# Two-layer RWKV-7 and stick-breaking trunk: another substitution, RWKV's keys in whole rows, memory block moved, new order

## The chip, the cores and the metric

One core of one Trainium2 chip runs the whole program, one launch. The time is the device time of that launch in microseconds (us), the median of several runs. TensorE is called PE here, its weight loads PEld, VectorE DVE, ScalarE ACT, GpSimd POOL and SyncE SP.

## The reference, cut to what matters

256 tokens of 1024 channels go through two layers. Each layer is a gated FFN, a mixer with cross-attention to 256 memory tokens, and a second FFN, each closed by a layer norm. The mixer of layer 0 is RWKV-7, that of layer 1 stick-breaking attention.

```python
# layer i
x = LN(alpha * x + 0.5 * swiglu_1(x))            # (silu(x @ w_gate) * (x @ w_up)) @ w_down, D_FF = 2816
p = x @ W_in[i]                                  # token-mixer columns | memory-query columns
h = concat(mixer(p_mix), memory_attention(p_memq, memK, memV))
x = LN(alpha * x + h @ W_out[i])
x = LN(alpha * x + 0.5 * swiglu_2(x))

mem_kv = mem @ w_mem_kv                          # once, 1024 -> 256 keys | 256 values; 4 heads of 64
memory_attention: softmax(q @ memK.T / 8) @ memV

rwkv7:  kk = k * k_k;  kk = kk / |kk| per head;  k = k * (1 + (a - 1) * k_a)
        per token: state = state * w - (state @ kk) (kk * a)^T + v k^T;  out = state @ r
stick-breaking: att[t, s] = exp(log_sigmoid(z[t, s]) - sum over later s' < t of softplus(z[t, s'])), z = q k / 8
```

The kernel computes the token recurrence of RWKV in chunks of 64 tokens. Inside a chunk, the rows depend on each other through a unit lower triangular matrix of 64 x 64 per head, which has to be inverted. It does so for blocks of 16 x 16 by forward substitution, for 96 blocks at once (128 partitions, one block in each), and for the larger blocks by products on PE.

## The kernel before, in words

The tokens stand in two halves of 128 (`half 0`, `half 1`; tiles x_78 and x_79). All weights are streamed from HBM through SP's queue in pieces of 128 x 1024 (`piece`, ring `raw` of 8 tiles). Each piece is split in two numbers of reduced precision: ACT copies it to a `hi` tile, DVE subtracts to get `lo` (`lo = raw - hi`), both in rings of 9 tiles. A product is then three matmuls (`mm3`): hi by hi, lo by hi, hi by lo. In the rows, `hi_7r`, `lo_8r` and the like are such pieces, xTh and xTl the turned activations in two parts.

An FFN column block is 256 of the 2816 hidden columns (`ffn_block`, 11 of them). It is "alone" when it is computed for one half only (24 matmuls of 512 columns for gate and up, 12 for down, 2 transpositions), or for both halves at once from one load of its weights (96 matmuls of 256 columns, 24 of 512 for down). PSUM banks: ps_2, ps_3 for transpositions ("tp"), ps_29, ps_30 for gate and up and for projections ("gu"), ps_25 and ps_26 the accumulators of half 0, ps_27 and ps_28 of half 1; the mixers also use the accumulator banks.

What runs when: in layer 0, half 0 gets five alone columns and six shared ones, `memory_kv` stands among the first blocks, then the norm of half 0. While half 0 goes through the mixer, half 1 gets the columns that it still lacks (`alternate`, lag1); while half 1 goes through the mixer, half 0 is in its second FFN (lag2). The columns of the other half are thus what PE does while a mixer's chain is on DVE and ACT. HEAD, LAGS, FIRST, HOLD and TAIL say how many alone columns stand at each place.

The order on each engine is not that of the code. `Plan` records all operations, then `order` lists them: of the operations that can start soonest, within AHEAD ns of the soonest on that engine, the one with the lowest rank. The rank is the place in the code, plus WAIT per ns of waiting, plus SWITCH where ACT would need another table, plus TURN where PE changes its mode; operations of a mixer's chain stand BOOST earlier. `improve` then tries changed places, from a SEED.

`memory_kv` (L806) loads the memory rows of each half by itself, turns them in groups of four (two splits of 512 each), loads the pieces of w_mem_kv once and multiplies half after half in one gu bank.

In the mixer of layer 0, `rwkv` (L911), the tiles are named by slots: Sk, L, Lm, T, Tt, RB, Y, lb, qr, kn, vn, bn. Three places are touched:

- the keys (L984 on): `t1 = (a - 1) * k_a`, the square of `k * k_k`, and the two products with it, each as one operation per group of 128 channels (NT = 6 groups),
- the substitution (L1098 to L1102): for each k of 0 to 14 one product of column k of L with row k of the inverse T, into `lb`, and one subtraction from the rows below, in `Tt`. In the rows these are the pairs `lb<-Y,Tt` and `Tt<-Tt,lb`, with 15 to 64 elements per partition,
- the copy of the memory queries `mq`.

In layer 1, `stick` (L1267) computes the logarithms: Exp, then Ln of the sums, in the tiles L, Lm, T and Tt of 768 columns; then Exp of the attention in qr and Sk. Exp (with Tanh) and Ln lie in different activation tables, so ACT_TABLE_LOAD stands between them.

## Time and profile before

| | |
|---|---|
| median of 3 runs | 1133.79 us (1130.95 to 1135.38) |
| the profiled execution's own time | 1131.83 us |
| its span in the trace | 1129.7 us |
| PE busy | 1075.0 us (95%), 7013 instructions |
| PEld busy | 903.4 us (80%) |
| DVE busy | 955.0 us (85%), 1426 instructions |
| ACT busy | 739.3 us (65%), 991 instructions |
| read from HBM | 304.22 MB |
| chain that ended last | PE 83%, DVE 12%, issue 2%, DMA 2%, ACT 1% |

The span lies 2.1 us below the profiled execution's time; the trace doesn't show those. A busy time counts each instruction from start to end, and neighbours on an engine overlap a little, so a sum of durations is more than the time that they took. The norm statistics on DVE (BN_STATS) mark where one part ends: 170.8 us (half 0, FFN 1 of layer 0), 289.8 (half 1), 324.5 and 495.0 (both halves behind the mixer of layer 0), 589.7 and 624.4 (FFN 2), 769.4 and 854.1 (FFN 1 of layer 1), 886.6 and 976.0 (behind stick-breaking), 1099.7 and 1120.3 (FFN 2).

### The profile page before, as it was taken

What the parts mean: (1) busy time and instruction counts of PE and PEld (TensorE: products, weight loads), DVE (VectorE), ACT (ScalarE), POOL (GpSimd) and SP (SyncE); (2) the same over time, 40 slices, a digit from 0 to 9 for tenths busy, and PEclk for the clock granted to TensorE, in tenths of its full rate; (3) what the DMA queues carried; (4) which work ended last, traced back from release to release, by engine and by line L of the source; (5) the groups of instructions that cost most, each with busy time, mean ns of one, the idle gap of its engine ahead of it and who ended that gap; (6) DMA issues with size and microseconds to landing.
All of it is one profiled execution on the core that took longest, in us unless ns stands there. A gap on an engine that the chain in (4) does not pass through costs nothing.

```text
span 1129.7 us, 19266 instructions
## 1 busy us (share of the span) xinstructions
PE 1075.0 (95%) x7013; PEld 903.4 (80%) x7013; DVE 955.0 (85%) x1426; ACT 739.3 (65%) x991; POOL 2.7 (0%) x14
## 2 busy tenths in 40 slices
...
GB/s 357 252 183 379 246 237 294 304 191 116 178 219 305 150 160 258 260 350 365 329 289 329 301 286 257 234 242 261 383 258 266 342 292 271 373 342 326 277 277 113
DMA packets 214721, 306.55 MB, mean 271 GB/s; under 512 B 14004, under 2 KB 161632, under 8 KB 214626
## 3 DMA queue, kind: packets, MB, share of 16 engines
...
HBM read 304.22 MB, written 1.05 MB: 270 GB/s over the span
## 4 chain that ended last, share of the span: by engine, by line
PE 83%; DVE 12%; issue 2%; DMA 2%; ACT 1%; SPq 0%; DVEq 0%; ACTq 0%
PE ps_29r L562 25%; PE ps_30r L562 25%; PE ps_28r L562 7%; PE ps_27r L562 7%; PE ps_26r L562 7%; PE ps_25r L562 7%; PE ps_2r L562 3%; PE ps_3r L562 3%; DVE Y_377r L562 1%; DVE Tt_366r L562 1%; DVE lo_17r L562 1%; DVE lo_35r L562 1%; DVE lo_14r L562 1%; DVE lo_23r L562 1%; DMA raw_9r<-in_ffn_w_up_dram 1%
## 5 line engine op out<-in xcount | busy, mean ns | idle before, releaser
L562 ACT ACTIVATE h_32r<-ps_30r 128x256 f32<-128x256 f32 (+1 forms) x50 | 21.1, 421 | 30.3 <-PE ps_30r L562 29.8
L562 ACT ACTIVATE h_33r<-ps_29r 128x256 f32<-128x256 f32 (+1 forms) x48 | 20.0, 416 | 31.1 <-PE ps_29r L562 30.8
L562 DVE TENSOR_TENSOR h_33r<-h_33r,ps_29r 128x256 f32<-128x256 f32 x31 | 13.0, 418 | 11.3 <-ACT h_33r L562 11.1
L562 ACT ACTIVATE hi_19r<-raw_15r 128x1024 fp32r<-128x1024 f32 x13 | 13.7, 1056 | 9.3 <-DMA raw_15r<-in_w_out_dram 3.7
L562 PE MATMUL ps_30r<-hi_16r,xTh 128*128 128x512 f32 x46 | 19.7, 428 | 0.0
L562 PE MATMUL ps_30r<-lo_17r,xTh 128*128 128x512 f32 x46 | 18.1, 393 | 1.0 <-DVE lo_17r L562 1.0
L562 PE MATMUL ps_2r<-cst,x 128*128 128x128 f32 x48 | 9.2, 325 | 10.3 <-DMA x<-in_x_dram 5.3
L562 DVE TENSOR_TENSOR lo_20r<-raw_15r,hi_19r 128x1024 fp32r<-128x1024 f32 x13 | 15.8, 1216 | 3.4 <-ACT hi_19r L562 3.4
L562 PE MATMUL ps_30r<-hi_16r,xTl 128*128 128x512 f32 x46 | 18.0, 392 | 0.0
L562 PE MATMUL ps_29r<-lo_14r,xTh 128*128 128x512 f32 x26 | 10.9, 419 | 7.1 <-DVE lo_14r L562 7.1
L562 PE MATMUL ps_30r<-hi_10r,xTh 128*128 128x512 f32 (+1 forms) x42 | 17.5, 416 | 0.0
L562 PE MATMUL ps_29r<-hi_22r,xTh 128*128 128x512 f32 x42 | 17.4, 415 | 0.0
L562 ACT ACT_TABLE_LOAD x13 | 16.7, 1283 | 0.9 <-PEq L1451 0.7
L562 ACT ACTIVATE hi_16r<-raw_36r 128x1024 fp32r<-128x1024 f32 x10 | 10.6, 1057 | 10.2 <-DMA raw_36r<-in_w_out_dram 9.0
L562 ACT ACTIVATE hi_22r<-raw_9r 128x1024 fp32r<-128x1024 f32 x12 | 12.8, 1063 | 6.8 <-PE ps_30r L562 3.9
L562 DVE TENSOR_TENSOR lo_23r<-raw_9r,hi_22r 128x1024 fp32r<-128x1024 f32 x12 | 14.6, 1218 | 3.0 <-ACT hi_22r L562 3.0
L562 PE MATMUL ps_30r<-lo_11r,xTh 128*128 128x512 f32 (+1 forms) x42 | 16.5, 394 | 0.3 <-DVE lo_11r L562 0.3
L562 PE MATMUL ps_29r<-hi_22r,xTl 128*128 128x512 f32 x42 | 16.6, 396 | 0.0
L562 PE MATMUL ps_29r<-lo_23r,xTh 128*128 128x512 f32 x42 | 16.6, 395 | 0.0
L562 PE MATMUL ps_30r<-hi_10r,xTl 128*128 128x512 f32 (+1 forms) x42 | 16.5, 392 | 0.0
L562 PEld LDWEIGHTS ps_2r<-cst,x 128*128 128x128 f32 x48 | 6.8, 166 | 11.8 <-issue 5.3
L562 DVE TENSOR_TENSOR lo_35r<-raw_12r,hi_34r 128x1024 fp32r<-128x1024 f32 x12 | 14.6, 1216 | 1.9 <-ACT hi_34r L562 1.9
...
## 6 DMA issues: line engine op xcount, KB each, us to landing
...
```

What stands on the lines that cost most here:

```text
L562: fn(*[at(x) for x in a], **{n: at(x) for n, x in k.items()})
```

## The change

- **Numbers of the plan.** The numbers below; with LAGS[1] one column of layer 1's first FFN is shared instead of computed alone for each half.
- **The memory block.** `memory_kv` is a generator: it loads the memory rows into tiles of the ring `raw`, the turned parts lie in tiles of the rings `hi` and `lo`, and each piece of w_mem_kv serves both halves, with one gu bank each. It stands behind the norm of half 0 now, ahead of the RWKV chain of half 0.
- **Scale.** The 1/8 of the memory scores is in the copy of mq, and the maximum is taken with the sign turned, so one operation of two elements falls away per bank.
- **Keys.** The operations per group of 128 channels become one of 768 channels, with the factor broadcast; the square is taken of a product that DVE writes first.
- **Substitution.** The 16 x 16 block is taken as two 8 x 8 blocks on its diagonal, both in one operation: 7 steps of two operations. The block below the diagonal follows from two products of 8 x 8 x 8 (512 elements each) and two reductions.

```diff
-HEAD = 2
-LAGS = ((5, 9), (5, 8))
-FIRST = 1
+HEAD = 1
+LAGS = ((5, 9), (4, 8))
+FIRST = 2
-HOLD = (2, 3)
+HOLD = (3, 4)
-TAIL = (2, 2)
-AHEAD = dict(PE=100.0, DVE=400.0, ACT=0.0)
-WAIT = 0.98
-SWITCH = 49.0
-BOOST = 18.375
+TAIL = (1, 2)
+AHEAD = dict(PE=100.0, DVE=200.0, ACT=0.0)
+WAIT = 7.6832
+SWITCH = 68.6
+BOOST = 12.8625
-SEED = 201
-TURN = 11760.0
+SEED = 144
+TURN = 23520.0
...
     def memory_kv():
-        mT = []
+
+        rows = [new(wp, [P, D], F32, "raw", "mem", NRAW) for _ in range(NHALF)]
+        for hf, mt in enumerate(rows):
+            nc.in_turn("load", nc.sync.dma_start(mt, mem[0, half_sl(hf), :]))
+        o = [ps("gu") for _ in range(NHALF)]
+        for g in range(2):
+            mT = [new(wp, [P, D], F32R, n, "mT", NPIECE).rearrange("p (s k t) -> p s k t", s=NHALF, t=P) for n in ("hi", "lo")]
+            for hf, mt in enumerate(rows):
+                to_T(mt[:, g * 512:(g + 1) * 512], [t[:, hf] for t in mT], 0, 4)
+            for k, h, l in cols_pieces(w_mem_kv, 0, 512, (2 * g, 2 * g + 1)):
+                for hf in range(NHALF):
+                    mm3(o[hf], mT[0][:, hf, k % 4], mT[1][:, hf, k % 4], h, l, k == 0, k == KT - 1)
+                yield
...
-            nc.vector.tensor_reduce(rs[:, 0, two], scv, AX.X, ALU.max)
-            nc.vector.tensor_scalar(rs[:, 0, two], rs[:, 0, two], -0.125, None, ALU.mult)
+            nc.vector.tensor_reduce(rs[:, 0, two], scv, AX.X, ALU.max, negate=True)
...
-                nc.vector.tensor_copy(mq, ptv[:, nt:n // P])
+                nc.vector.tensor_scalar(mq, ptv[:, nt:n // P], 0.125, None, ALU.mult)
...
-        for j in range(NT):
-            nc.vector.tensor_scalar(t1[:, j], a[:, j], 1.0, k_a[:, j:j + 1], ALU.subtract, ALU.mult)
+        nc.vector.scalar_tensor_tensor(t1, a, 1.0, bc(k_a, 2, [P, NT, P]), ALU.subtract, ALU.mult)
...
-        for j in range(NT):
-            nc.scalar.activation(sq[:, 0, j], zk[:, j], AF.Square, scale=k_k[:, j:j + 1])
+        nc.vector.tensor_tensor(bt, zk, bc(k_k, 2, [P, NT, P]), ALU.mult)
+        nc.scalar.activation(sq[:, 0], bt, AF.Square)
...
-        for j in range(NT):
-            for dst, w in ((cv4(qr[:, :, 0]), e1[:, :, :, 0:C]), (cv4(bt), cv4(a))):
-                nc.vector.scalar_tensor_tensor(dst[:, j], cv4(zk)[:, j], k_k[:, j:j + 1], w[:, j], ALU.mult, ALU.mult)
+        nc.vector.tensor_mul(cv4(qr[:, :, 0]), cv4(bt), e1[:, :, :, 0:C])
+        nc.vector.tensor_mul(bt, bt, a)
...
-        for k in range(BLK - 1):
-            n = BLK - 1 - k
-            sh = [P, n, k + 1]
-            nc.vector.tensor_tensor(tmp[:, :n, :k + 1], bc(Lb[:, k, k + 1:], 2, sh), bc(Tn[:, k, :k + 1], 1, sh), ALU.mult)
-            nc.vector.tensor_tensor(Tn[:, k + 1:, :k + 1], Tn[:, k + 1:, :k + 1], tmp[:, :n, :k + 1], ALU.subtract)
+        for k in range(hb8 - 1):
+            n = hb8 - 1 - k
...
+            nc.vector.tensor_tensor(t, col, row, ALU.mult)
+            low = duo(Tn, k + 1, n, 0, k + 1)
+            nc.vector.tensor_tensor(low, low, t, ALU.subtract)
...
+        nc.vector.tensor_tensor(terms, bc(Lb[:, lo8, hi8].rearrange("p k i -> p i k"), 2, cube),
+                                bc(Tn[:, lo8, lo8].rearrange("p k j -> p j k"), 1, cube), ALU.mult)
+        nc.vector.tensor_reduce(w8, terms, AX.X, ALU.add, negate=True)
+        nc.vector.tensor_tensor(terms, bc(Tn[:, hi8, hi8], 2, cube), bc(w8.rearrange("p k j -> p j k"), 1, cube), ALU.mult)
+        nc.vector.tensor_reduce(Tn[:, hi8, lo8], terms, AX.X, ALU.add)
...
-            memory_kv()
...
+        if i == 0:
+            run(memory_kv())
```

The plan then orders the instructions anew. Three places follow, each with the order before and now.

DVE, memory block. Before, it stands among the first FFN columns; mT are the turned memory rows, memV and memKT the values and the turned keys.

```order
L562 TENSOR_TENSOR mT_58r<-ps_3r,mT_57r 128x512
L562 TENSOR_TENSOR lo_8r<-raw_9r,hi_7r 128x1024
L562 TENSOR_TENSOR lo_20r<-raw_12r,hi_19r 128x1024
L562 TENSOR_TENSOR mT_61r<-ps_2r,mT_60r 128x512
L562 TENSOR_TENSOR lo_23r<-raw_15r,hi_22r 128x1024
L562 TENSOR_TENSOR lo_11r<-raw_18r,hi_10r 128x1024
L562 COPY memV<-ps_30r 128x256
L562 TENSOR_TENSOR lo_14r<-raw_21r,hi_13r 128x1024
L562 TENSOR_TENSOR mT_65r<-ps_3r,mT_64r 128x512
L562 TENSOR_TENSOR mT_68r<-ps_2r,mT_67r 128x512
L562 COPY memKT<-ps_3r 128x2x128
```

Now it stands behind the norm of half 0; the turned rows are the four operations of 512 that read ps_2 and ps_3 and write lo_35 and lo_17.

```order
L562 TENSOR_TENSOR lo_41r<-raw_39r,hi_40r 128x1024
L562 TENSOR_TENSOR lo_23r<-raw_9r,hi_22r 128x1024
L562 TENSOR_TENSOR lo_14r<-raw_21r,hi_13r 128x1024
L562 TENSOR_TENSOR lo_35r<-ps_3r,hi_34r 128x512
L562 TENSOR_TENSOR lo_11r<-raw_15r,hi_10r 128x1024
L562 TENSOR_TENSOR lo_35r<-ps_2r,hi_34r 128x512
L562 TENSOR_TENSOR lo_17r<-ps_3r,hi_16r 128x512
L562 TENSOR_TENSOR lo_8r<-raw_18r,hi_7r 128x1024
L562 TENSOR_TENSOR lo_20r<-raw_36r,hi_19r 128x1024
L562 TENSOR_TENSOR lo_17r<-ps_2r,hi_16r 128x512
L562 TENSOR_TENSOR lo_38r<-raw_39r,hi_37r 128x1024
L562 TENSOR_TENSOR lo_35r<-raw_9r,hi_34r 128x1024
```

The same splits of turned rows stand in another part of the program, among splits of weight pieces.

DVE, substitution of half 1, from its first step. Before:

```order
L562 TENSOR_TENSOR lb_506r<-Y_377r,Tt_366r 128x15
L562 TENSOR_TENSOR Tt_366r<-Tt_366r,lb_506r 128x15
L562 TENSOR_TENSOR lb_506r<-Y_377r,Tt_366r 128x14x2
L562 TENSOR_TENSOR Tt_366r<-Tt_366r,lb_506r 128x14x2
L562 TENSOR_TENSOR lb_506r<-Y_377r,Tt_366r 128x13x3
L562 TENSOR_TENSOR Tt_366r<-Tt_366r,lb_506r 128x13x3
L562 TENSOR_TENSOR lb_506r<-Y_377r,Tt_366r 128x12x4
```

Now (slots have other numbers: lb is lb_480, Tt is Tt_340, Y is Y_351):

```order
L562 TENSOR_TENSOR lb_480r<-Y_351r,Tt_340r 128x14
L562 TENSOR_TENSOR lo_17r<-raw_18r,hi_16r 128x1024
L562 TENSOR_TENSOR Tt_340r<-Tt_340r,lb_480r 128x2x7
L562 SCALAR_TENSOR_TENSOR h_32r<-h_32r,ps_30r 128x256
L562 TENSOR_TENSOR lb_480r<-Y_351r,Tt_340r 128x24
L562 TENSOR_TENSOR lo_8r<-raw_24r,hi_7r 128x1024
L562 TENSOR_TENSOR Tt_340r<-Tt_340r,lb_480r 128x2x6x2
L562 TENSOR_TENSOR lo_11r<-raw_39r,hi_10r 128x1024
L562 TENSOR_TENSOR lb_480r<-Y_351r,Tt_340r 128x30
L562 TENSOR_TENSOR xTl<-ps_28r,xTh 128x2x128
L562 TENSOR_TENSOR Tt_340r<-Tt_340r,lb_480r 128x2x5x3
L562 TENSOR_TENSOR RB_344r<-ps_27r,cst 128x6x64
```

Before, the steps stand one behind the other; now another operation stands between every two of them.

ACT, the logarithms of stick-breaking half 1, up to the first Exp of the attention (qr). Before:

```order
L562 ACT_TABLE_LOAD
L562 ACTIVATE L_382r<-L_382r 128x768
L562 ACTIVATE Lm_367r<-Lm_367r 128x768
L562 ACTIVATE T_376r<-T_376r 128x768
L562 ACTIVATE hT_1974r<-ps_2r 128x256
L562 ACTIVATE hi_10r<-raw_21r 128x1024
L562 ACTIVATE Tt_366r<-Tt_366r 128x768
L562 ACTIVATE hi_7r<-raw_12r 128x1024
L562 ACTIVATE hi_22r<-raw_24r 128x1024
L562 ACTIVATE hi_13r<-raw_9r 128x1024
L562 ACT_TABLE_LOAD
L562 ACTIVATE qr_56r<-qr_56r 128x384 x2
```

Now (L is L_356, Lm is Lm_341, T is T_350, Tt is Tt_340, qr is qr_390):

```order
L562 ACT_TABLE_LOAD
L562 ACTIVATE L_356r<-L_356r 128x768
L562 ACT_TABLE_LOAD
L562 ACTIVATE T_350r<-T_350r 128x768
L562 ACT_TABLE_LOAD
L562 ACTIVATE Lm_341r<-Lm_341r 128x768
L562 ACTIVATE hi_13r<-raw_21r 128x1024
L562 ACTIVATE T_350r<-T_350r 128x768
L562 ACT_TABLE_LOAD
L562 ACTIVATE h_33r<-ps_29r 128x256
L562 ACTIVATE hi_22r<-raw_18r 128x1024
L562 ACT_TABLE_LOAD
```

Two table loads stand in the rows of before; in those of now there are five, and a sixth follows ahead of the first Exp of qr.

## Rows read from the trace of the kernel before

**Rows 1.** windows between norms: us, busy us by engine, PEclk, DMA share, GB/s

```profile
0.00:170.80 170.80, 160.71 (x987) 143.58 (x988) 111.25 (x127) 97.81 (x123) 1.63 (x9) 1.00 0.79 276
170.80:289.80 119.00, 111.43 (x1016) 89.90 (x1015) 114.56 (x236) 84.54 (x135) 0.20 (x1) 0.96 0.67 226
289.80:324.50 34.70, 25.87 (x275) 21.74 (x274) 33.15 (x68) 11.72 (x17) 0.64 (x3) 0.80 0.53 165
324.50:495.00 170.50, 158.43 (x1358) 125.66 (x1357) 163.30 (x305) 113.05 (x169) 0.21 (x1) 0.96 0.72 238
...
769.40:854.10 84.70, 83.36 (x405) 64.94 (x404) 77.91 (x106) 71.66 (x95) 0.00 (x0) 1.00 0.88 307
...
886.60:976.00 89.40, 89.29 (x472) 69.60 (x471) 87.26 (x118) 75.46 (x101) 0.00 (x0) 1.00 0.89 298
```

**Rows 2.** waits of PE, by releaser: us in total, times, longest us

```profile
PE ps_29r L562 <- DVE lo_14r L562: 7.1, 2, 6.0
PE ps_2r L562 <- DVE lb_506r L562: 5.9, 1, 5.9
PE ps_26r L562 <- DVE Y_377r L562: 5.8, 1, 5.8
...
PE ps_3r L562 <- DVE mT_65r L562: 2.1, 1, 2.1
```

**Rows 3.** chain that ended last, in order of time: start us, us, what

```profile
62.02 1.44 PE ps_30r L562 x12
...
65.25 5.47 PE ps_30r L562 x24
```

**Rows 4.** timeline of DVE, memory block: start us, us, operation

```profile
46.66 0.68 DVE L562 TENSOR_TENSOR mT_65r<-ps_3r,mT_64r 128x512 fp32r<-128x512 f32 x1
47.26 0.68 DVE L562 TENSOR_TENSOR mT_68r<-ps_2r,mT_67r 128x512 fp32r<-128x512 f32 x1
```

**Rows 5.** timeline of DVE, RWKV keys of half 0

```profile
206.66 0.34 DVE L562 SCALAR_TENSOR_TENSOR L_382r<-h_33r,vc,pT_399r 128x128 f32<-128x128 f32 x1
206.92 0.28 DVE L562 TENSOR_SCALAR Sk_381r<-RB_370r,vc 128x128 f32<-128x128 f32 x1
207.11 0.34 DVE L562 SCALAR_TENSOR_TENSOR L_382r<-h_33r,vc,pT_399r 128x128 f32<-128x128 f32 x1
...
213.21 0.96 DVE L562 TENSOR_TENSOR RB_370r<-RB_370r,Y_377r 128x768 f32<-128x768 f32 x1 [0.16 <-ACT Y_377r L562]
214.08 0.34 DVE L562 SCALAR_TENSOR_TENSOR qr_56r<-L_382r,vc,T_376r 128x128 f32<-128x128 f32 x1
```

**Rows 6.** timeline of DVE, substitution, half 0 and (from 402.86) half 1

```profile
255.99 0.18 DVE L562 TENSOR_TENSOR lb_506r<-Y_377r,Tt_366r 128x15 f32<-128x15 f32 x1
...
267.16 0.16 DVE L562 TENSOR_TENSOR Tt_366r<-Tt_366r,lb_506r 128x15 f32<-128x15 f32 x1
...
402.86 0.19 DVE L562 TENSOR_TENSOR lb_506r<-Y_377r,Tt_366r 128x15 f32<-128x15 f32 x1
...
407.78 0.22 DVE L562 TENSOR_TENSOR lb_506r<-Y_377r,Tt_366r 128x55 f32<-128x55 f32 x1
407.91 0.41 DVE L562 SCALAR_TENSOR_TENSOR h_33r<-h_33r,ps_29r 128x256 f32<-128x256 f32 x1
...
408.82 1.22 DVE L562 TENSOR_TENSOR lo_20r<-raw_21r,hi_19r 128x1024 fp32r<-128x1024 f32 x1
409.96 0.20 DVE L562 TENSOR_TENSOR Tt_366r<-Tt_366r,lb_506r 128x48 f32<-128x48 f32 x1
...
412.74 0.15 DVE L562 TENSOR_TENSOR Tt_366r<-Tt_366r,lb_506r 128x15 f32<-128x15 f32 x1
```

**Rows 7.** timeline of ACT, logarithms of stick-breaking half 1

```profile
931.66 1.28 ACT L562 ACT_TABLE_LOAD   x1
932.96 0.85 ACT L562 ACTIVATE L_382r<-L_382r 128x768 f32<-128x768 f32 x1
...
941.37 0.94 ACT L562 ACTIVATE qr_56r<-qr_56r 128x384 f32<-128x384 f32 x2
```

More of the change, by code (lines that the diff above doesn't have):

```diff
@@ L806, in memory_kv @@
     def memory_kv():
-        mT = []
-        for hf in range(NHALF):
-            mt = sl("qr", [P, D])
-            nc.sync.dma_start(mt, mem[0, half_sl(hf), :])
-            for g in range(2):
-                t = tuple(new(mp, [P, 4, P], F32R, n, "mT") for n in
-                          (("vn", "bn"), ("kn", "RB"), ("L", "Lm"), ("T", "Tt"))[2 * hf + g])
-                to_T(mt[:, g * 512:(g + 1) * 512], t, 0, 4)
-                mT.append(t)
-        pieces = cols_pieces(w_mem_kv, 0, 512)
-        for hf in range(NHALF):
-            a = ps("gu")
-            for k, h, l in pieces:
-                th, tl = mT[2 * hf + k // 4]
-                mm3(a, th[:, k % 4], tl[:, k % 4], h, l, k == 0, k == KT - 1)
+        rows = [new(wp, [P, D], F32, "raw", "mem", NRAW) for _ in range(NHALF)]
[10 more added lines that the diff above has]
+                yield
+        for hf in range(NHALF):
             mk = new(tp_, [P, MEMW], F32, "ta", "mk", 2)
-            nc.scalar.activation(mk, a[:, :MEMW], AF.Copy)
-            nc.vector.tensor_copy(memV[:, hf], a[:, MEMW:])
+            nc.scalar.activation(mk, o[hf][:, :MEMW], AF.Copy)
+            nc.vector.tensor_copy(memV[:, hf], o[hf][:, MEMW:])
             pt = ps("tp")
-            for j in range(2):
-                nc.tensor.transpose(pt[:, j * P:(j + 1) * P], mk[:, j * P:(j + 1) * P], ident)
+            with nc.together():
+                for j in range(2):
+                    nc.tensor.transpose(pt[:, j * P:(j + 1) * P], mk[:, j * P:(j + 1) * P], ident)
             nc.vector.tensor_copy(memKT[:, :, half_sl(hf)], pt[:, :2 * P].rearrange("p (j t) -> p j t", t=P))
@@ L841, in mem_attention @@
             two = slice(2 * p, 2 * p + 2)
-            nc.vector.tensor_reduce(rs[:, 0, two], scv, AX.X, ALU.max)
-            nc.vector.tensor_scalar(rs[:, 0, two], rs[:, 0, two], -0.125, None, ALU.mult)
+            nc.vector.tensor_reduce(rs[:, 0, two], scv, AX.X, ALU.max, negate=True)
             e = new(tp_, [P, 2, SEQ], F32, "ta", "e", 2)
             for j in range(2):
-                nc.scalar.activation(e[:, j], scv[:, j], AF.Exp, bias=rs[:, 0, 2 * p + j:2 * p + j + 1], scale=0.125,
+                nc.scalar.activation(e[:, j], scv[:, j], AF.Exp, bias=rs[:, 0, 2 * p + j:2 * p + j + 1],
                                      accum_out=rs[:, 1, 2 * p + j:2 * p + j + 1])
@@ L1080, in rwkv @@
         X, Tn = tt[:, :512], tt[:, 512:].rearrange("p (i j) -> p i j", j=BLK)
-        tmp = sl("lb")[:, :256].rearrange("p (i j) -> p i j", j=BLK)
+        scratch = sl("lb")
+        tmp = scratch[:, :256]
         D4 = v4(Dd, True)
```

12 lines of the change are left out of this document (11 added, 1 removed).

## The prediction

> **What bounds the kernel now.** I read the windows between the layer norms first, since the program runs from one norm of a half of x to the next and every edit lies between two known ones. The bounds of the windows are the starts of the norm statistics on DVE. Up to 170.8 us (the first FFN, all eleven columns for half 0 and six of them for half 1 too, and the memory block) PE is busy 160.7 us and DVE 111.3 [rows 1]: PE sets that time. From 170.8 to 495.0 us lie both RWKV halves. There DVE is busy 114.56 + 33.15 + 163.30 = 311.0 of 324.2 us (96%), PE 111.43 + 25.87 + 158.43 = 295.7: PE has 28.5 us without work, and where it idles most, from 289.8 to 324.5, its granted clock is .80 on average instead of 1.00 [rows 1]. The waits say the same: three long ones of PE, 6.0, 5.9 and 5.8 us, end with a DVE write (a weight split, the scratch lb of the substitution, Y of the triangular part), and one of 2.1 us with the split of the turned memory rows [rows 2]. So in the RWKV stretch DVE sets the time, and PE everywhere else: from 769.4 to 854.1 us PE is busy 83.36 of 84.70, from 886.6 to 976.0 us 89.29 of 89.40 [rows 1].
>
> **How I count.** For an engine that sets the time I take the number of its instructions between two norms in the order that the program prints, times the distance from start to start in the trace (neighbours overlap, so the duration of one is too much). On PE: 24 matmuls of 512 columns in 5.47 us, .2267 each, and 12 of 256 columns in 1.44 us, .120 each [rows 3]; a transposition of 128 columns I set at .108, a little under the .120. On DVE: a 1024 split 1.14 (408.82 to 409.96), a 512 one .60 (46.66 to 47.26), a 768 product .87 (213.21 to 214.08), a 128 scalar_tensor_tensor .26 and a 128 tensor_scalar .19 (206.66, 206.92, 207.11) [rows 4 to 6].
>
> **Up to the first norm: -15.4 us.** Memory_kv leaves this part, and the FFN columns in it stay as they are: up to the last matmul of half 0's first accumulator there are 312 instead of 360 matmuls of 512 columns, 26 instead of 46 transpositions of 128, and 576 of 256 columns in both. That is 48 x .2267 + 20 x .108 = 13.0, with rounding 13.1 us less on the engine that sets the time. The wait of PE for mT, 2.1 us [rows 2], goes with the block; with the slower matmuls just behind it I put 2.3. What hides this saving: only DVE (97 instead of 105 us of counted work, far below) and the weights' transfers, which lose 3 MB of the block too.
>
> **RWKV stretch: +6.5 us.** Here the block arrives, on the engine that sets the time. Counted from the first norm's statistics to half 1's second, DVE's work:
> - memory block: 4 splits of 1024 x 1.14 + 4 of 512 x .60 + 4 copies of 256 at .35 (an estimate between the .26 of 128 elements and the .60 of 512) = +8.4; two copies of mq become two tensor_scalar of the same size, nothing;
> - 2 more splits of 1024, of pieces whose matmuls lie elsewhere: +2.3;
> - RWKV keys, both halves: -12 tensor_scalar x .19 - 24 scalar_tensor_tensor of 128 x .26 + 8 operations of 768 x .87 = -2.3 - 6.2 + 7.0 = -1.5. The six Squares on ACT become one behind a new DVE product (ACT now waits for bt); ACT has 30% of its time free, and the next user is rn, so I put that at nothing: DVE's queue covers it with splits;
> - substitution, both halves: -60 small operations + 28, which at the distance of neighbours that don't depend on each other (.13, 407.78 to 407.91 [rows 6]) is -7.8 + 3.6; plus 4 products of 512 x .60 and 4 reductions to 64 of 512 elements. Such a reduction isn't in the trace; between .50 (its elements at the 768 row's .87) and .95, I take .61: +4.8. Sum +.6;
> - the rest (four negations of two elements gone, single gate operations that cross a norm) about 0.
>
> Sum +9.3: 298.3 us of counted work become 307.6. Before, 324.2 - 298.3 = 25.9 us were not work. Part of this is dependence: in the substitution each step reads the one ahead, and 20 steps from 402.86 to 407.78 took .246 each instead of .13 [rows 6]. In the new order nearly every two steps have a split or another piece of work between them (ahead: the order of half 1), and in the whole stretch 88 instead of 113 neighbours on DVE depend on each other: 25 x .11 = -2.8. So +9.3 - 2.8 = **+6.5**. Bounds: the wasted share stays as it was (324.2/298.3 = 1.087): 307.6 x 1.087 - 324.2 = +10.1; half of the 25.9 go, because PE gets 9.4 us more work here and can be fed while DVE is in a chain: 307.6 + 12.9 - 324.2 = -3.7. I take the middle, since the trace shows dependence at DVE but not that its other waits depend on the order.
>
> **Behind RWKV: +2.8 us.** PE's counted work here: 33 fewer matmuls of 512, 96 more of 256, 2 fewer of 128 (HOLD, TAIL, FIRST and LAGS give other columns to both halves at once): -7.5 + 11.5 - .2 = +3.8, in full, as PE sets this part. From 769.4 to 854.1 us PE's count was 78.7 us of 84.7; DVE, busy 77.91 us there [rows 1], has 14 us less of counted work in the new order (77 to 63), and PE 67.3 instead of 78.7. I take half of the 6 us of slowness: -3 (bounds 0 and -6). Last, **activation tables**: in stick-breaking half 1 ACT switches between Ln and Exp six times instead of twice. A load and the way to the next ACTIVATE take 931.66 to 932.96, 1.30 us [rows 7]: 4 x 1.30 = 5.2 us more on ACT, and the chain from the first load to the first Exp, 9.7 us before (931.66 to 941.37), becomes 15.6: the four loads, and one Exp of 768 (.75) that stood ahead of the first load before. PE never idles in that window before [rows 1], with FFN columns as cover; whether they last 6 us longer can't be read. Bounds 0 and +5.2; I take +2, nearer to nothing because of the full row. If the cover is gone, the value product of half 1 waits and the norm behind it slips by the same.
>
> The Trainium skill, page "ScalarE: Activation LUTs" (What ACT_TABLE_LOAD costs; Table sets: the hidden batching unit), speaks against this order: do all of one set, then the other, as each switch costs the load and about as much again of drain, 2.66 us. By it, as an estimate, the four loads would be 10.6 us and not 5.2; the row has the next ACTIVATE 1.30 us behind the load's start, so the trace doesn't show the second half.
>
> SP issues 10 DMAs less, the 2 of the memory rows now through the ring of weight tiles, where the pieces behind them queue; DMA is busy 79% in the first window and 67% in the second [rows 1], so I put that at nothing.
>
> **Sum.** -15.4 + 6.5 + 2.8 = -6.1 us (2.8 = 3.8 - 3 + 2). The profiled execution took 1131.83 us, so 1125.7; the median of the runs is 1133.79, .17% above it: 1127.7, told as **1127**.
>
> **The rivals.**
> 1. *A larger gain.* The stretch ends at its lower bound (-3.7 instead of +6.5) and the logs stay covered (0 instead of +2): 1127.7 - 10.2 - 2 = 1115.5. For it: the three PE waits of about 6 us each [rows 2] are PE's, behind DVE chains that the new order cuts up. Against: DVE is at 96% there, and a cut chain doesn't lessen its work.
> 2. *The gain at the start is given back.* The stretch at 1.087 (+3.6 more), the table loads wholly on the path (+3.2 more), nothing won from 769 to 854 us (+3): 1137.5. For it: all four extra loads stand in one chain. Against: PE's full window. With the page's price and all of it on the path the forecast alone would be 1127.7 - 2 + 10.6 = 1136.3, the same side.
> 3. *Slower: the substitution's chain decides, not DVE's sum.* Steps that took 9.9 us in half 1 (402.86 to 412.74 [rows 6]) have 15.8 us of DVE work from first to last in the new order, 15.4 in half 0, where it took 11.3 (255.99 to the end of the last step at 267.32). What comes behind (the narrow products, the state, the output) is one chain, and it starts 5.8 + 4.1 = 9.9 us later. As long as DVE has splits to do behind the substitution this is only another order of the same work. It decides once the splits drawn forward are missing behind it, with nine tiles for pieces: then DVE and PE both wait. Price +9.9, dependence not saved +2.8: 1140.4; with part of the loads 1142.
> 4. That the change doesn't do what it says is excluded for the operations (they stand in the order); for the block's move it is rival 2.
>
> **Chances.** Forecast .48 (its own range 1121 to 1133), rival 1 .18, rival 2 .18, rival 3 .16. The measurement tells .5% (5.7 us) from no change: faster is under 1128.1, slower over 1139.5. The forecast lies near that edge: .30 of its .48 are faster, .18 the same. With rival 1 faster is .48; rival 2 and a part of rival 3 make same .39; the rest, .13, is slower. The range leaves out the lower half of rival 1 and the upper of rival 3: 1114 to 1141.
>
> **What would show it.** First norm's statistics at about 155.4 us (170.8 - 15.4): right if within 3 us. Half 1's second norm at 495.0 - 15.4 + 6.5 = 486.1; at 476 rival 1, at 490 rival 2, beyond 495 rival 3. PE's waits for mT and lb gone; DVE in the stretch 96% or more busy; lb, Tt steps about 16 us from first to last. In the log phase 15 to 16 us from first load to first Exp, and PE's idle there under 2 us. What would make me wrong: DVE idling in the stretch (then the sum doesn't set it), or a first part that DMA holds above 160 us.

## The result

The changed kernel takes 1121.97 us (median of 4 runs, 1121.43 to 1123.72) against 1132.37 us of the kernel before in the same session (four runs; the 1133.79 that the forecast started from is the median of three of them): the ratio is 0.9908 with a 95% interval of 0.9881 to 0.9934, so 10.4 us faster. The forecast was 1127 in a range of 1114 to 1141. The profiled execution took 1121.84 us, its span is 1120.0 (before 1129.7). Of the experiments below, one execution of r11_noalgebra took 2700.33 us, far from its other five, and is left out of its median.

Windows of the changed kernel between the norms, bounds again at the starts of the norm statistics; the columns are those of [rows 1], and the stretches answer to those rows one by one:

```profile
0.00:157.70 157.70, 148.76 (x919) 134.00 (x920) 102.21 (x115) 90.81 (x113) 1.62 (x9) 0.99 0.82 278
157.70:294.60 136.90, 130.99 (x1173) 105.40 (x1172) 129.96 (x232) 92.68 (x143) 0.20 (x1) 0.98 0.69 230
294.60:319.20 24.60, 17.96 (x181) 14.59 (x182) 23.99 (x54) 6.61 (x10) 0.63 (x3) 0.86 0.47 138
319.20:487.90 168.70, 158.19 (x1369) 123.61 (x1368) 165.94 (x280) 116.89 (x169) 0.20 (x1) 1.00 0.78 255
...
768.30:837.90 69.60, 69.18 (x350) 55.49 (x349) 64.14 (x88) 56.81 (x77) 0.00 (x0) 1.00 0.92 318
...
870.60:957.40 86.80, 83.73 (x449) 64.69 (x448) 81.91 (x112) 77.37 (x103) 0.00 (x0) 1.00 0.86 291
```

The first norm comes 13.1 us earlier (157.7 for 170.8). The RWKV stretch, from the first norm of half 0 to the second of half 1, takes 330.2 us instead of 324.2, 6.0 more; DVE is busy 129.96 + 23.99 + 165.94 = 319.9 us in it (97%). Behind it, 632.1 us instead of 634.7: 2.6 less. The sum is -9.7 on the span.

Busy time of the engines of the changed kernel over the whole span, and then the stretch alone, before and now:

```profile
PE 1072.2 (96%) x7057; PEld 900.9 (80%) x7057; DVE 944.5 (84%) x1357; ACT 734.0 (66%) x979; POOL 2.7 (0%) x14
```

```profile
170.80:495.00 324.20, 295.73 (x2644) 237.30 (x2643) 311.00 (x607) 209.31 (x319) 1.05 (x5) 0.94 0.68 226
157.70:487.90 330.20, 307.14 (x2720) 243.60 (x2719) 319.89 (x565) 216.18 (x322) 1.04 (x5) 0.98 0.72 236
```

PE is busy 2.8 us less than before (1075.0) and without work for 47.8 us instead of 54.7. In the stretch its granted clock is .98 on average instead of .94.

Waits of PE in the changed kernel, as in [rows 2]: us in total, times, longest us.

```profile
PE ps_2r L562 <- DMA x<-in_x_dram: 5.2, 1, 5.2
PE ps_3r L562 <- DVE x L562: 5.1, 1, 5.1
PE ps_3r L562 <- DVE L_356r L562: 3.4, 1, 3.4
PE ps_25r L562 <- ACT Tt_340r L562: 2.9, 1, 2.9
...
PE ps_2r L562 <- DVE lb_480r L562: 1.0, 1, 1.0
```

The three waits of about 6 us on a split, on lb and on Y are gone, and so is mT. But PE's time without work in the stretch falls only from 28.5 to 23.1 us. A wait of 5.1 us for x, behind the norm of half 1, has come into it:

```profile
306.37 1.11 PE L562 MATMUL ps_3r<-cst,x 128*128 128x128 f32 x4 [5.06 <-DVE x L562]
```

The next longest there is 2.9 us for Tt from ACT; lb is left with 1.0, and the rest are many small ones.

What such a wait cost before shows at the first of them, 256.3 to 262.3 us (columns as in [rows 1]):

```profile
256.30:262.30 6.00, 0.00 (x0) 0.00 (x0) 5.35 (x22) 0.51 (x2) 0.00 (x0) 0.69 0.03 13
262.30:268.80 6.50, 6.49 (x38) 4.72 (x39) 6.50 (x20) 2.55 (x4) 0.00 (x0) 0.50 0.34 122
```

PE stood still, its granted clock fell from 2.4 to 1.2 GHz during the wait, and it stayed at 1.2 (.50) for 6.5 us of work behind it. At the other two waits it was the same, for 4.8 and 3.3 us of work. So a wait costs PE more than its length.

DVE in the substitution of half 0, as in [rows 6]:

```profile
249.01 0.17 DVE L562 TENSOR_TENSOR lb_480r<-Y_351r,Tt_340r 128x14 f32<-128x14 f32 x1
249.22 0.19 DVE L562 TENSOR_TENSOR Tt_340r<-Tt_340r,lb_480r 128x14 f32<-128x14 f32 x1
...
249.65 0.18 DVE L562 TENSOR_TENSOR lb_480r<-Y_351r,Tt_340r 128x24 f32<-128x24 f32 x1
249.74 1.22 DVE L562 TENSOR_TENSOR lo_17r<-raw_21r,hi_16r 128x1024 fp32r<-128x1024 f32 x1
250.88 0.18 DVE L562 TENSOR_TENSOR Tt_340r<-Tt_340r,lb_480r 128x24 f32<-128x24 f32 x1
...
259.32 1.03 DVE L562 TENSOR_TENSOR lb_480r<-Y_351r,Tt_340r 128x512 f32<-128x512 f32 x1
260.27 0.55 DVE L562 TENSOR_TENSOR Sk_355r<-ps_3r,cst 128x384 f32<-128x384 f32 x1
260.74 0.67 DVE L562 TENSOR_REDUCE lb_480r<-lb_480r 128x64 f32<-128x512 f32 x1
261.33 1.21 DVE L562 TENSOR_TENSOR lo_11r<-raw_36r,hi_10r 128x1024 fp32r<-128x1024 f32 x1
262.47 1.16 DVE L562 TENSOR_TENSOR lb_480r<-Tt_340r,lb_480r 128x512 f32<-128x512 f32 x1
263.55 1.22 DVE L562 TENSOR_TENSOR lo_14r<-raw_39r,hi_13r 128x1024 fp32r<-128x1024 f32 x1
264.68 0.68 DVE L562 TENSOR_REDUCE Tt_340r<-lb_480r 128x64 f32<-128x512 f32 x1
```

From the first step to the end of the last it takes 16.4 us (249.01 to 265.36), longer than the 11.3 of before, and 16 other operations stand between the 18 (before, 9 between the 30). The two products of 512 take .95 (259.32 to 260.27) and 1.08 us (262.47 to 263.55) from start to start, where I counted .60; the reduction .59 (260.74 to 261.33), where I counted .61.

### The profile page after: what moved, and what is told of

Read it like the earlier page. It is cut to its first block, busy times and chain, and to the rows that moved or that the text cites. A ratio compares the mean times of both kernels' runs of the same rounds, so it can differ in the third digit from the quotient of the medians.

```text
span 1120.0 us, 19287 instructions
## 1 busy us (share of the span) xinstructions
PE 1072.2 (96%) x7057; PEld 900.9 (80%) x7057; DVE 944.5 (84%) x1357; ACT 734.0 (66%) x979; POOL 2.7 (0%) x14
## 4 chain that ended last, share of the span: by engine, by line
PE 58%; DVE 11%; ACT 2%; issue 2%; DMA 2%; SPq 0%; DVEq 0%; ACTq 0%
PE ps_30r L562 17%; PE ps_29r L562 17%; PE ps_27r L562 6%; PE ps_28r L562 6%; PE ps_25r L562 4%; PE ps_26r L562 4%; PE ps_3r L562 2%; PE ps_2r L562 2%; DVE x L562 1%; DVE S_104r L562 1%; ACT L562 1%; DVE lo_41r L562 1%; DVE Y_351r L562 0%; DVE lb_480r L562 0%; DVE lo_14r L562 0%
## 5 line engine op out<-in xcount | busy, mean ns | idle before, releaser
L562 ACT ACT_TABLE_LOAD x17 | 21.8, 1283 | 1.0 <-PEq L1466 0.7
L562 PE MATMUL ps_30r<-hi_22r,xTh 128*128 128x512 f32 x50 | 20.9, 418 | 0.0
L562 PE MATMUL ps_30r<-lo_23r,xTh 128*128 128x512 f32 x50 | 19.6, 391 | 0.0
L562 PE MATMUL ps_30r<-hi_22r,xTl 128*128 128x512 f32 x50 | 19.5, 391 | 0.0
L562 ACT ACTIVATE hi_19r<-raw_12r 128x1024 fp32r<-128x1024 f32 x13 | 13.8, 1060 | 6.8 <-PE ps_28r L562 3.0
L562 DVE TENSOR_TENSOR h_33r<-h_33r,ps_29r 128x256 f32<-128x256 f32 x32 | 13.3, 416 | 5.0 <-ACT h_33r L562 4.8
L562 DVE TENSOR_TENSOR lo_20r<-raw_12r,hi_19r 128x1024 fp32r<-128x1024 f32 x13 | 15.8, 1218 | 1.7 <-DMA raw_18r<-in_ffn_w_up_dram 1.6
L562 PE MATMUL ps_29r<-hi_34r,xTh 128*128 128x512 f32 x40 | 16.4, 411 | 0.7 <-DVE h_32r L562 0.7
L562 ACT ACTIVATE hi_37r<-raw_39r 128x1024 fp32r<-128x1024 f32 x11 | 11.6, 1056 | 8.2 <-DMA raw_39r<-in_rwkv_w_in_dram 6.4
L562 PE MATMUL ps_29r<-hi_7r,xTh 128*128 128x512 f32 (+1 forms) x42 | 16.2, 386 | 0.0
L562 PE MATMUL ps_29r<-lo_35r,xTh 128*128 128x512 f32 x40 | 15.8, 394 | 0.5 <-DVE lo_35r L562 0.5
L562 ACT ACTIVATE hi_34r<-raw_21r 128x1024 fp32r<-128x1024 f32 x11 | 11.6, 1058 | 7.0 <-DMA raw_21r<-in_rwkv_w_in_dram 2.8
L562 PE MATMUL ps_29r<-hi_7r,xTl 128*128 128x512 f32 (+1 forms) x42 | 16.0, 380 | 0.0
L562 PE MATMUL ps_29r<-lo_8r,xTh 128*128 128x512 f32 (+1 forms) x42 | 16.0, 380 | 0.0
L562 PE MATMUL ps_29r<-hi_34r,xTl 128*128 128x512 f32 x40 | 15.7, 392 | 0.0
```

Of the source, the lines that this page charges most:

```text
L562: fn(*[at(x) for x in a], **{n: at(x) for n, x in k.items()})
```

## The experiments

All were compared with the kernel before on the same chip. Two kinds have to be kept apart. In r1 to r6, r9 and r11 the plan orders everything anew, and that order is different in many places. In r7, r8, r10 and r12 the order is kept and one thing is moved or exchanged in it.

The table has, for each, the ratio to the kernel before with its interval, the first norm, the RWKV stretch, in it DVE's work counted as in the prediction (each instruction at its distance from start to start) and what is left over, and the time behind the stretch. What is left over is the sum of all distances beyond the counted ones; where the text says lost to dependence, it is that sum over neighbours of which the second reads what the first wrote. All columns from the fourth on are of one profiled execution.

| kernel | median us | ratio (95%) | first norm | stretch | DVE work | left | behind |
|---|---|---|---|---|---|---|---|
| before | 1131 to 1132 | | 170.8 | 324.2 | 298.3 | 25.9 | 634.7 |
| changed | 1121.97 | .9908 (.9881 to .9934) | 157.7 | 330.2 | 307.6 | 22.6 | 632.1 |
| r1_block | 1129.01 | .9976 (.9965 to .9986) | 156.7 | 335.8 | 306.1 | 29.7 | 633.9 |
| r2_algebra | 1132.48 | 1.0002 (.9992 to 1.0013) | 173.2 | 319.8 | 297.4 | 22.4 | 636.2 |
| r3_numbers | 1122.21 | .9915 (.9899 to .9931) | 170.5 | 317.9 | 300.6 | 17.3 | 630.9 |
| r4_seed | 1126.82 | .9956 (.9942 to .9971) | 170.6 | 318.5 | 297.8 | 20.7 | 635.4 |
| r5_columns | 1131.47 | .9994 (.9983 to 1.0005) | 169.5 | 320.1 | 298.3 | 21.8 | 639.2 |
| r6_weights | 1128.86 | .9972 (.9959 to .9985) | 171.3 | 319.3 | 298.3 | 21.0 | 632.9 |
| r7_logs | 1119.40 | .9890 (.9875 to .9906) | 157.7 | 330.2 | 307.6 | 22.6 | 629.3 |
| r8_gather | 1130.04 | .9981 (.9970 to .9992) | 157.2 | 336.0 | 307.6 | 28.4 | 632.5 |
| r9_noblock | 1120.33 | .9897 (.9881 to .9913) | 171.0 | 310.8 | 293.8 | 17.0 | 636.7 |
| r10_steps | 1122.89 | .9916 (.9901 to .9931) | 157.2 | 329.7 | 307.1 | 22.6 | 632.8 |
| r11_noalgebra | 1127.70 | .9956 (.9940 to .9971) | 157.8 | 327.2 | 302.9 | 24.3 | 638.6 |
| r12_both | 1121.28 | .9909 (.9894 to .9924) | 170.6 | 310.9 |  |  | 637.0 |

The profiled execution of r6_weights (1125.37 us), r8_gather (1127.51) and r11_noalgebra (1125.46) was the fastest of its kernel, 2 to 4 us below the median, so those columns show these three a little too short.

The theory that came out of the prediction (A): the memory block leaves the part that PE sets, and what it costs in the stretch is less. The rival (B): the new order makes the gain, whatever the block does.

### The parts alone: r1_block, r2_algebra, r3_numbers, r4_seed

r1_block is the kernel before with `memory_kv` of the change and its new place:

```diff
-            memory_kv()
...
+        if i == 0:
+            run(memory_kv())
```

> The kernel before with the memory block alone changed: both halves per weight piece, moved behind the first norm; old keys, old substitution, old numbers. The plan orders everything anew. Theory A (the gain is the block leaving the part that PE sets): first norm about 157 us instead of 170.8, the RWKV stretch about 6 to 9 us longer, time 5 to 7 us below the kernel before. Rival B (the gain is whatever order the plan happens to find): no more below the kernel before than the run with another seed, 0 to 3 us.

Its three windows (up to the first norm, the stretch, behind it):

```profile
0.00:156.70 156.70, 149.62 (x921) 135.02 (x922) 103.10 (x115) 90.84 (x113) 1.62 (x9) 1.00 0.81 282
156.70:492.50 335.80, 306.98 (x2714) 245.05 (x2713) 318.93 (x620) 215.77 (x330) 1.04 (x5) 0.95 0.69 227
492.50:1126.40 633.90, 617.63 (x3381) 520.86 (x3379) 531.53 (x694) 429.86 (x551) 0.00 (x0) 1.00 0.86 294
```

The start gives 14.1 us, as expected; the stretch takes back 11.6. 2.7 us remain by the medians: rival B's 0 to 3, not theory A's 5 to 7. DVE's work rises by 7.8 us and what is left over by 3.8.

r2_algebra is the kernel before with the new keys, substitution and scale:

```diff
-        for k in range(BLK - 1):
+        for k in range(hb8 - 1):
...
-            nc.vector.tensor_scalar(t1[:, j], a[:, j], 1.0, k_a[:, j:j + 1], ALU.subtract, ALU.mult)
+        nc.vector.scalar_tensor_tensor(t1, a, 1.0, bc(k_a, 2, [P, NT, P]), ALU.subtract, ALU.mult)
```

> The kernel before with keys in whole rows, substitution by pairs of 8x8, and the scale in the copy of mq; block and numbers as before. Theory A: DVE's sum in the stretch falls by about 1 us for keys and substitution together and 2 to 3 us of dependence go, so 1 to 4 us below the kernel before. Rival C (the chain of the substitution, about 10 us a half, was on the path): its steps fall from 30 to 18, so 5 us or more below.

No change, so neither theory A's 1 to 4 us nor rival C's 5: the stretch is 4.4 us shorter, but the start 2.4 and the rest 1.5 longer.

r3_numbers has all the new numbers, and no other edit:

```diff
-HEAD = 2
+HEAD = 1
...
-WAIT = 0.98
+WAIT = 7.6832
...
-SEED = 201
+SEED = 144
```

> The kernel before with the new numbers of the plan alone (HEAD, LAGS, FIRST, HOLD, TAIL, AHEAD, WAIT, SWITCH, BOOST, SEED, TURN). Theory A: one column is shared (3 fewer loads of weights), PE's sum is the same: within 3 us of the kernel before. Rival B: 5 us or more below, since the order makes the gain.

1122.21 us: the numbers alone give all that the whole change gives, with the block at its old place and the old substitution. That is rival B's side.

r4_seed changes the seed alone:

```diff
-SEED = 201
+SEED = 144
```

> The kernel before with another seed of the plan's search and nothing else: how far one order differs from another with the same work. Theory A: within 3 us of the kernel before. Rival B: differences of 5 us and more are usual, and the change's gain can't be told from them.

Another draw of the search alone makes 5.0 us (median 1126.82 against 1131.8, ratio times 1131.8). In the stretch, the same DVE work (297.8 for 298.3) ends 5.7 us earlier. So theory A falls: the block alone is worth a quarter of the gain, and two orders of the same work differ by more than that. One other seed was tried, so how far orders scatter is not known beyond this 5.0. It also limits what any of the freshly ordered kernels can prove: a difference under some 5 us can be the draw.

### Which numbers: r5_columns, r6_weights

The numbers are of three kinds: counts of columns (HEAD, LAGS, FIRST, HOLD, TAIL), weights of the plan (AHEAD, WAIT, SWITCH, BOOST, TURN) and the seed. Theory D, formed on the first four: the plan's weights make an order in which DVE wastes less of the stretch, and the block is worth little. Its rival E: the other counts of columns do it.

```diff
-HEAD = 2
-LAGS = ((5, 9), (5, 8))
-FIRST = 1
+HEAD = 1
+LAGS = ((5, 9), (4, 8))
+FIRST = 2
...
-HOLD = (2, 3)
-TAIL = (2, 2)
+HOLD = (3, 4)
+TAIL = (1, 2)
```

> The kernel before with the new counts of columns alone (HEAD, LAGS, FIRST, HOLD, TAIL), the plan's weights and seed as before. The numbers together were worth 9.6 us, 6.4 of it in the RWKV stretch and 3.8 behind it. Theory D (the weights make the order that DVE wastes less in; the columns act behind RWKV alone): 2 to 4 us below the kernel before, stretch at about 324 us. Rival E (the columns make the gain: they give PE other work to hide behind): 7 us or more below, stretch at 318.

No change (ratio .9994), less than either theory said; the stretch is 4.1 us shorter and the rest 4.5 longer.

```diff
-AHEAD = dict(PE=100.0, DVE=400.0, ACT=0.0)
-WAIT = 0.98
-SWITCH = 49.0
-BOOST = 18.375
+AHEAD = dict(PE=100.0, DVE=200.0, ACT=0.0)
+WAIT = 7.6832
+SWITCH = 68.6
+BOOST = 12.8625
...
-TURN = 11760.0
+TURN = 23520.0
```

> The kernel before with the plan's new weights alone (AHEAD, WAIT, SWITCH, BOOST, TURN); columns and seed as before. Theory D: 5 to 7 us below the kernel before, DVE's wasted time in the stretch 17 to 20 us instead of 25.9, with fewer neighbours that depend on each other (88 instead of 112). Rival E: within 2 us of the kernel before. Rival B (scatter from order to order, about 5 us as with the other seed): nothing fixed, anything between 0 and 6 below, without the fewer neighbours mattering.

3.2 us (ratio .9972), half of what theory D expected, with 97 neighbours on DVE in the stretch that depend on each other instead of 112. Columns, weights and seed alone make .7 + 3.2 + 5.0 = 8.9 us, together 9.6. How much of it the numbers cause and how much is the draw, these runs don't separate.

### The order held: r8_gather

In the changed kernel's own order, the 18 operations of a substitution move forward to the place of the first; their readers stay.

```diff
         order = self.improve()
+        for steps in self.steps:
+            mine = [x for x in order if x[2].i in steps]
+            at0 = order.index(mine[0])
+            order = [x for x in order if x[2].i not in steps]
+            order[at0:at0] = mine
...
```

> The changed kernel with the 18 substitution operations of each half pulled together to where the first stands, so that the splits between them come behind; all else stands as it was, and the readers of the result too. Theory D (interleaving saves DVE the dependence of the steps): about .11 x 17 = 2 us a half more on DVE, and splits come up to 5 us later for PE: 3 to 6 us slower than the changed kernel. Rival F (interleaving is worth nothing, the sum of work counts): within 1.5 us of it.

DVE there (first step, last step, first split behind), and then the two longest waits of PE:

```profile
248.59 0.17 DVE L567 TENSOR_TENSOR lb_480r<-Y_351r,Tt_340r 128x14 f32<-128x14 f32 x1
...
254.53 0.69 DVE L567 TENSOR_REDUCE Tt_340r<-lb_480r 128x64 f32<-128x512 f32 x1
...
255.46 1.22 DVE L567 TENSOR_TENSOR lo_17r<-raw_21r,hi_16r 128x1024 fp32r<-128x1024 f32 x1
```

```profile
PE ps_2r L567 <- DVE h_32r L567: 7.4, 1, 7.4
PE ps_30r L567 <- DVE lo_17r L567: 6.7, 1, 6.7
```

The substitution is done in 6.6 us instead of 16.4, and the kernel is 8 us slower (ratio .9981 for .9908; the intervals don't touch). In the profiles it is 5.7 us, all of it in the stretch. The split lo_17 begins at 255.46 instead of 249.74, and PE waits 6.7 us for it; in half 1 it waits 7.4 for a gate. Two of the three long waits that [rows 2] show of before are of this kind. Rival F (within 1.5 us) fails. In the profile theory D's 3 to 6 us hold, by the medians it is more. Of the 5.8 us that DVE has left over in addition, 3.6 are dependence (121 neighbours in the stretch that depend on each other lose 11.6 us, against 8.0 with 88); the rest is DVE waiting. That this comes with PE's late columns is not shown. The steps stand closer here than they did before, where 9 others stood among the 30, so the 8 us are not what the old order lost by it.

### The substitution itself: r10_steps

The old 30 operations in the places of the 18 new ones, the order held:

```diff
...
+        slots = nc.ops[step0:]
+        for j, o in enumerate(slots):
+            mine = old[j:j + 1] if j < 14 else old[14 + 4 * (j - 14):18 + 4 * (j - 14)]
+            o.calls = [(nc.real.vector.tensor_tensor, x, {}) for x in mine]
```

> The changed kernel in its own order, with the old substitution put where the new one stands: the 30 operations of 15 steps lie in the places of the 18 new ones, one each in the first 14, four each in the last 4. By the sum of DVE's work (30 x .13 against 14 x .10 and 4 x .61, equal) only 12 more dependent neighbours a half count, .11 each: 1 to 3 us slower than the changed kernel. Rival C (the new form of the substitution is itself worth much): 5 us or more slower.

.9 us by the medians, within the intervals, and nothing in the profile (stretch 329.7 for 330.2). The new form of the substitution is worth nothing here, and rival C falls. By the counts (307.1 us of DVE work for 307.6), what it saves in steps the two products of 512, at about 1 us each, cost.

### The change less one part: r9_noblock, r11_noalgebra

r9_noblock is the changed kernel with the old `memory_kv` at its old place:

```diff
+            memory_kv()
...
-        if i == 0:
-            run(memory_kv())
```

> The changed kernel without the block: memory_kv in its old form at its old place; new numbers, keys and substitution; ordered anew. The block alone brought 14.1 us at the start and cost 11.5 in the stretch. Theory D (the order makes the gain and the block is worth 0 to 3 us): within 3 us of the changed kernel, with the first norm at 170 us and the stretch at 314 to 320 instead of 330. Theory A, the one of the prediction (the block is the gain): 8 to 13 us slower than the changed kernel.

```profile
0.00:171.00 171.00, 162.93 (x987) 145.64 (x988) 110.47 (x126) 96.99 (x123) 1.64 (x9) 1.00 0.79 273
171.00:481.80 310.80, 287.67 (x2626) 230.83 (x2625) 303.44 (x548) 205.26 (x306) 1.04 (x5) 0.97 0.72 237
481.80:1118.50 636.70, 621.94 (x3448) 527.80 (x3446) 525.99 (x686) 427.42 (x548) 0.00 (x0) 0.99 0.85 288
```

1120.33 us, as fast as the changed kernel: 13.3 us later at the first norm, 19.4 us less in the stretch and 4.6 more behind it. Moving the block was worth nothing that shows on top of the numbers; theory A wanted 8 to 13 us, more than the 5.0 by which the other seed moved the time.

r11_noalgebra leaves the block and the numbers and takes the old keys, substitution and scale:

```diff
-        nc.vector.scalar_tensor_tensor(t1, a, 1.0, bc(k_a, 2, [P, NT, P]), ALU.subtract, ALU.mult)
+        for j in range(NT):
+            nc.vector.tensor_scalar(t1[:, j], a[:, j], 1.0, k_a[:, j:j + 1], ALU.subtract, ALU.mult)
...
```

> The changed kernel without the algebra: old keys, substitution and scale; block moved, new numbers; ordered anew. Theory D: within 3 us of the changed kernel (algebra alone was worth nothing, scatter of orders 5 us). Rival C: 5 us or more slower.

5.4 us slower by the ratios and 3.7 in the profile, where neither theory fits well: the algebra alone was worth nothing (r2), and the substitution in a held order nothing (r10). The stretch is 3.0 us shorter and the rest 6.6 longer, which the keys and the substitution of RWKV don't touch. It can be the draw (5 us), but no run holds the order for the keys, so it stays open.

### The table loads: r7_logs, r12_both

The four logarithms of stick-breaking half 1 one behind the other, the order held:

```diff
...
+        lns = [x for x in act if x[2].func == "Ln"][-4:]
+        between = act[act.index(lns[0]):act.index(lns[-1])]
+        early = [x for x in between if x[2].func == "Exp"] + lns
+        order = [x for x in order if x not in early[:-4] + lns[1:]]
...
```

> The changed kernel with one thing moved in its order: in stick-breaking half 1 all four logarithms stand one behind the other, the last Exp ahead of them, so 4 of the 17 activation table loads fall away; all else stands as it was. If the loads lie on the path as predicted: 2 us faster (up to 5.2). If FFN columns cover them: no change, within 1 us. By the Trainium skill's price (ScalarE: Activation LUTs, What ACT_TABLE_LOAD costs), as an estimate and on the path: 10.6 us.

ACT in the changed kernel, then in r7_logs (table loads, first logarithm, first Exp of the attention), and the window of r7_logs that answers to 870.60 above:

```profile
917.04 1.28 ACT L562 ACT_TABLE_LOAD   x1
918.33 0.85 ACT L562 ACTIVATE L_356r<-L_356r 128x768 f32<-128x768 f32 x1
919.20 1.28 ACT L562 ACT_TABLE_LOAD   x1
...
931.90 1.28 ACT L562 ACT_TABLE_LOAD   x1
933.19 0.94 ACT L562 ACTIVATE qr_390r<-qr_390r 128x384 f32<-128x384 f32 x2
```

```profile
917.89 1.28 ACT L569 ACT_TABLE_LOAD   x1
919.18 0.85 ACT L569 ACTIVATE L_356r<-L_356r 128x768 f32<-128x768 f32 x1
...
923.20 1.28 ACT L569 ACT_TABLE_LOAD   x1
...
927.62 0.92 ACT L569 ACTIVATE qr_390r<-qr_390r 128x384 f32<-128x384 f32 x2
```

```profile
870.70:954.40 83.70, 83.19 (x449) 64.86 (x448) 81.87 (x112) 71.75 (x99) 0.00 (x0) 1.00 0.89 303
```

First load to first Exp: 16.2 us in the changed kernel, 9.7 in r7_logs. The window is 83.7 us instead of 86.8, PE's idle time in it .5 instead of 3.1, and every other norm keeps its distance within .2 us. So the four extra loads, with the Exp that stood between them, cost 3.0 us in the profile, 2.6 by the medians of the two sessions and 2.0 by the ratios. 1119.40 us is the lowest of all; its interval (.9875 to .9906) overlaps that of the changed kernel (.9881 to .9934), so the gain rests on the profile.

r12_both makes the same move in r9_noblock's order, where two of 15 loads go:

```diff
...
+        early = [x for x in between if x[2].func == "Exp"] + lns
+        order = [x for x in order if x not in early[:-4] + lns[1:]]
...
```

> The kernel r9_noblock (changed kernel without the block) with the four logarithms of stick-breaking half 1 one behind the other, so 2 of its 15 activation table loads fall away; all else in its order. The 4 loads of the changed kernel cost 2.6 us together, .65 each. If each load on that chain costs the same: 1.3 us below r9_noblock, about 1119 us. If a load is on the path wholly or not at all: 2.6 us (2 x 1.30), or nothing.

Nothing (1121.28 us; the intervals overlap): span 1118.5 in both, and no window differs by more than .4 us. There the two loads didn't lie on the path.

## Why the prediction held, and where its reason did not

The time fell within the range and on the right side; the sum was -6.1 and the kernel made -10.4. The range, 1114 to 1141, also held no change at all (1133.8), so the hit by itself says little, and the sum came near partly by luck: its steps were off by +2.3, -.5 and -5.4 us. By steps:

- **First part, -15.4; measured -13.1.** The count of PE's work (13.0) came out to .1, partly by luck: PE's busy time fell by 12.0 us and its time without work by 1.1. The 2.3 for the mT wait failed: the wait is gone, but PE idles 1.0 us between 50 and 75 us, where it idled nothing, and its granted clock in the first 25 us is .93 instead of 1.00; that these two took the time back is not shown by a run.
- **RWKV stretch, +6.5; measured +6.0.** The 307.6 of DVE's work is the same count in the same order, so what was tested is the rest: 22.6 us, where 23.1 (25.9 less 2.8) was forecast. It came near because errors cancel. Dependence fell by 3.7 us (11.7 to 8.0) and not by 2.8, and the other waiting of DVE by 1.2, which was put at nothing. Against that, the products of 512 were mis-sized, 1.0 instead of .60 each: 4 x .4 = 1.6 us more, hidden in the 22.6. Two slips in the working changed nothing: the listed items add up to 9.8 and not 9.3, and +6.5 is not the middle of the bounds, which is 3.2. The bounds of the reduction had no good source (.87 for 768 gives .58 for 512, not .50).
- **Behind RWKV, +2.8; measured -2.6.** This is the step that failed. The +3.8 of PE was counted to the last accumulator matmul in PE's order. By the clock, PE passed 834 matmuls of 512 columns in the stretch instead of 778, 56 more and not 33: it was further on in the columns of the next FFN when the stretch ended. 23 x .2267 = 5.2 us that I had put behind the stretch were done in it. PE is busy 307.1 us there, 11.4 more than before. Counted by the clock the term is -1.6 and not +3.8; with -2 and +3 for the two below, that makes -.6, and 2.0 us of the -2.6 stay unexplained.
- **Tables, +2 of 0 to 5.2; measured 2.0 to 3.0** (r7). The chain of 15.6 us was 16.2, and PE's idle time in that window, put at under 2 us, was 3.1. The row priced the load: 1.29 us from a load to the next ACTIVATE (917.04 to 918.33). By the price of the Trainium skill (ScalarE: Activation LUTs, What ACT_TABLE_LOAD costs) 10.6 us, as an estimate, would have gone with the four loads, were they all on the path; the runs don't show that.
- **769 to 854 us, -3; measured about -2**: recounted by the clock at the median distance of each kind of matmul, PE's time beyond its counted work in that window fell from 3.1 to 1.0 us. Before, it was not the 6.0 that the prediction started from. The window itself got shorter mostly because its columns lie elsewhere.
- **Rival 3** (a longer substitution chain decides) had it the wrong way round: the chain did grow to 16.4 us, and pulling it together costs 8 us (r8). In r3_numbers the steps span 17.8 and 27.5 us, and that kernel is 9.6 us faster than the one before.
- **Rival 2** was right in one place: part of the table loads lay on the path. **Rival 1** had the right mark, the three waits of 6 us: they went, but other waits came (5.1 us for x), and PE had the block's work to do in the stretch besides.

What didn't hold is the reason behind the sum. I took the block's move for the gain (-15.4 + 8.4) and the order for a small correction (-2.8). Measured one by one, the block gives 14.1 and takes 11.6 (r1), and without it the kernel is as fast (r9); the numbers give 9.6 (r3). That the total came out near is, by these figures, because both changes reclaim the same waste: 25.9 us are left over before, 17.3 with the numbers alone, 22.6 with block and numbers together.

A count of PE over the whole program would have shown it ahead of the run. It does 48 matmuls of 512 less, 96 of 256 more and 4 transpositions less: -10.9 + 11.5 - .4 = +.2 us. Moving the block only moves work of an engine that is busy 95% of the span. So the 9.7 us can't be work that went. By PE's busy time they are its waits, 6.9 us, and some 3 us of matmuls that ran slowly. By the granted clock of the three windows of the stretch, PE stood at 1.2 GHz for some 37 us of it before and some 13 now.

That DVE alone sets the stretch, as the prediction has it, the runs don't show. The chain that ended last has DVE for 95 us of the stretch of before and PE for 205. Between r9_noblock and the changed kernel the stretch differs by 19.4 us and PE's busy time in it by 19.5, DVE's counted work by 13.8. In all the runs DVE stands idle in the stretch for 7 to 17 us and PE for 22 to 30: both are nearly full, and no run separates them.

What depends on the order is what is left over beyond DVE's work, 17 to 30 us; 6 to 12 of it are lost between neighbours that depend on each other. Interleaving the substitution is part of it: to undo it wholly, with the order held, costs 8.3 us by the ratios (r8). But the steps of the old order did not stand so close, so what share of the 10.4 us it made is open, and it is not the whole: r4_seed has hardly more between its steps than the kernel before (11 and 13 operations, for 9 and 9) and is 5.0 us faster, and r11_noalgebra, with 16 and 30, gains only 5.0.

Open: what part of the 9.6 us is the numbers and what part the draw of the search (one other seed was tried), what else in the order makes the gain, and what the keys are worth in a held order.
